# Head and product order of a split-fp32 trunk kernel: meta tokens transposed in one go, a regrouped third weight chunk, another bank for the taps, another table of products

## The chip, the cores and the metric

The kernel runs on one core of a Trainium2 chip. The metric is the device time of one execution in microseconds (us): the median over three timed runs. Lower is better. Where a single execution was profiled, its own time is given beside the span that the profiler saw.

## The reference

One layer of a decoder trunk over 16 learned meta tokens followed by 256 tokens of x, all in fp32, with D = 2048:

```python
h = concatenate([meta, x])                       # 272 x 2048
u = rms_norm(h, g_pre_mix)
z_pool, v, g, gate_a, gate_b = split(u @ w_in)   # 1024, 1024, 1024, 2048, 2048 columns
y_a = causal_multiscale_pool(z_pool, w_grp, scale) @ w_pool_out
c   = causal_depthwise_conv31(v * sigmoid(g), w_dw) + b_dw
y_b = silu(layer_norm(c, ln_g, ln_b)) @ w_conv_out
m = sigmoid(gate_a) * y_a + sigmoid(gate_b) * y_b
h = h + rms_norm(m @ w_o, g_post_mix)
h = h + rms_norm(relu(rms_norm(h, g_pre_mlp) @ w_up)**2 @ w_down, g_post_mlp)
return h[16:]
```

## The kernel before

**How a product is made.** An fp32 product is three matmuls of the type fp32r: the high part of the weights times the high and the low part of the activations, and the low part of the weights times the high part of the activations. The weights come from HBM in blocks of 1 MB (128 x 2048 fp32), issued by SyncE (SP, L733). ScalarE casts a block to its high part (`hi`, L754), VectorE subtracts that from the block (`lo`, L759), and TensorE uses both. `hi` and `lo` have three buffers each, so that a block is cast when the product three places earlier is done on TensorE.

**Which products there are.** After the head come the products of u with the columns of z, v and g ("Z"), the per-group map `grp`, and then a list of words in a table MAIN. A word such as `a13` is a plain product of a block of the stage a (gate_a) with all 256 tokens, 24 matmuls (stages: p pool projection, a and b the gates, c the conv projection, o the output projection). Words such as `a0P5` belong to a set of seven products in the manner of Strassen that stand for eight plain half-products; each is 12 matmuls. Some of the seven need a sum of two weight blocks. The table SUMMED says for which VectorE adds the two loaded blocks (L771); for the others GpSimd (POOL) issues an accumulating DMA from HBM on top of the block that lies in SBUF (L775), called a "bring" here. Other words of MAIN are steps: `fu` makes the token sums of the Strassen sets, `k1` hands two buffers (`raw_k`, in the place of the pooled activations `y`) to the weight loads once the pool projection is done on TensorE, `lnm` and `lnv` are the mean and the variance of the LayerNorm over c, `um8` hands over another buffer (`raw_um`), `OF` prepares the output projection.

**The order of the work.** TensorE takes the products in the order of MAIN. What VectorE, ScalarE, POOL and SP do is put in order ahead of time by a list scheduler (the class Plan) from written costs and due times; every engine then executes its own list in that order. The loads of SP are in the order in which blocks are first used, and a load waits until a buffer is free. VectorE's list mixes splits, sums, gate arithmetic and the 240 instructions of the depthwise conv ("taps", L886, 128x256 each), which must all be done before `lnm`.

**The head.** x comes in four blocks of 512 columns (`load_x`, L407): blocks 0 and 1 are issued by ScalarE's queue, 2 and 3 by SP between the weight chunks. The first two chunks (`raw_103`, `raw_109`) come in four pieces each. TensorE first does 14 dummy transposes (`keep_warm`, L430), one small transpose of g_pre_mix (L401) and 10 more dummies; then `x_tile` (L457) for column tiles k = 0 to 15: two 128x128 transposes of x (L461) and one of 16 meta rows (L462) into one PSUM tile, from which ScalarE (L463) makes the high and VectorE (L464) the low part of 272 columns of u. Between these transposes the loop multiplies the first chunk (`acc_v<-u_um`, L490), three tiles behind. ScalarE and VectorE split chunks 0, 1 and 2 in pieces of 128x256 meanwhile (`pieces_to`, L517), chunk 2 interleaved with chunk 1 in the last half. Four of the squares for the RMS norm (L472) go to odd k from 9 on.

**Rows and taps.** `rows_step` sums the squares over partitions into bank `y0` (L825), VectorE copies them to `rb` (L828); `taps_step` then transposes the rows of parameters into the same bank `y0` (L837) and the taps into `y1` (L841).

## Time and profile before

| | before |
|---|---|
| timed runs | 1197.83, 1196.41, 1196.10 us; median 1196.41 us |
| profiled execution, its own time | 1194.79 us |
| its span in the profile | 1193.0 us |
| mean granted TensorE clock | 0.997 |
| busy time of TensorE matmuls (PE) | 1172.1 us, 6324 instructions |
| busy time of VectorE (DVE) | 1076.1 us |
| busy time of ScalarE (ACT) | 710.4 us |
| busy time of GpSimd (POOL) | 54.6 us |
| DMA | 281.27 MB, 236 GB/s on average |

Busy times are of the whole span. In lists of instructions the first column is the start in us from the span's start, the second the time until the end of the last of the instructions in the row; "x14" at the end is how many instructions the row holds; brackets hold the idle time of the engine ahead of it and what ended it. The head reaches to about 48 us, the products of z, v and g to 161 us, the words of MAIN to 515 us; then come the two MLP products.

### The profile page before, as it was taken

To read this page: it belongs to the slowest core of one execution; us is meant where nothing else is said; L and a number is where in the kernel's file an instruction comes from. 1 tells how busy PE (TensorE), PEld (TensorE's weight loads), DVE (VectorE), ACT (ScalarE), POOL (GpSimd) and SP (SyncE) were. 2 spreads that over 40 slices of the span, in tenths; PEclk is the share of its full clock that TensorE was granted. 3 is DMA by queue.
4 is the path that set the end of the run, shared out by engine and by line. 5 is a ranking of instruction groups with operands and counts; after the bars stand their busy time and mean duration, and the time that the engine had idled before them with its cause. 6 is when DMAs were issued, how large, how long until landed. Compare 5 with 4: busy or idle time off the path is not lost.

```text
span 1193.0 us, 15777 instructions
## 1 busy us (share of the span) xinstructions
PE 1172.1 (98%) x6324; PEld 1013.9 (85%) x6324; DVE 1076.1 (90%) x1160; ACT 710.4 (60%) x718; POOL 54.6 (5%) x55
## 2 busy tenths in 40 slices
PE   9999999899999999999999999999999999999996
PEld 7999998788788878898888888888888888888885
DVE  5799999999988998787989989989999999899856
ACT  6633354565559656557776665666656756656542
POOL 1000000000000000000100000000000000000000
PEclk9999999999999999999999999999999999999998
DMA  9756444889856798549998897997998987979931
GB/s 310 230 177 212 142 141 141 237 258 268 249 187 212 176 388 258 196 128 345 236 342 225 246 317 179 262 309 191 300 276 211 304 239 234 317 181 266 331 140 70
DMA packets 181976, 281.27 MB, mean 236 GB/s; under 512 B 4641, under 2 KB 92129, under 8 KB 180992
## 3 DMA queue, kind: packets, MB, share of 16 engines
q1 hardware_dynamic: 160064, 235.09, 57.7%
q0 software_dynamic: 20688, 43.15, 19.9%
q10 hardware_dynamic: 1152, 2.04, 0.5%
q8 instruction: 49, 0.80, 0.3%
q14 instruction: 23, 0.19, 0.0%
HBM read 276.07 MB, written 4.19 MB: 235 GB/s over the span
## 4 chain that ended last, share of the span: by engine, by line
PE 78%; DVE 9%; DMA 7%; ACT 4%; issue 1%; ACTq 0%; DVEq 0%; SPq 0%
PE bank_u L495 16%; PE acc_up L1850 12%; PE bank_k L1166 11%; PE bank_u L501 8%; PE bank_k L490 7%; PE bank_a L1850 7%; PE bank_b L1850 5%; PE acc_v L490 4%; DVE lo L759 4%; PE acc_v L1166 4%; ACT hi L754 2%; DMA raw_p<-in_w_in_dram 2%; DMA kept<-h 1%; DVE c L886 1%; DVE raw_p L771 1%
## 5 line engine op out<-in xcount | busy, mean ns | idle before, releaser
L495 PE MATMUL bank_u<-m,hi 128*128 128x512 f32 x960 | 329.4, 390 | 0.0
L501 PE MATMUL bank_u<-m,lo 128*128 128x256 f32 x960 | 265.3, 276 | 0.0
L495 PEld LDWEIGHTS bank_u<-m,hi 128*128 128x128 f32 x960 | 180.2, 188 | 37.9
L754 ACT CAST hi<-raw_p 128x2048 fp32r<-128x2048 f32 x66 | 125.9, 1912 | 107.9 <-PE bank_k L1166 28.2
L501 PEld LDWEIGHTS bank_u<-m,lo 128*128 128x128 f32 x960 | 180.2, 188 | 1.6
L1676 DVE TENSOR_TENSOR lo<-raw_m,hi 128x2048 fp32r<-128x2048 f32 x71 | 162.4, 2287 | 15.2 <-ACT hi L1671 14.9
L1671 ACT CAST hi<-raw_m 128x2048 fp32r<-128x2048 f32 x71 | 135.8, 1913 | 52.0 <-PE bank_u L495 18.0
L759 DVE TENSOR_TENSOR lo<-raw_p,hi 128x2048 fp32r<-128x2048 f32 x66 | 150.4, 2287 | 15.6 <-ACT hi L754 15.4
L1850 PE MATMUL acc_up<-hi,forms 128*128 128x512 f32 x440 | 143.1, 390 | 1.0 <-ACT G L1875 1.0
L1671 ACT CAST hi<-raw_h 128x2048 fp32r<-128x2048 f32 x46 | 88.0, 1913 | 51.1 <-PE bank_u L495 32.0
L1676 DVE TENSOR_TENSOR lo<-raw_h,hi 128x2048 fp32r<-128x2048 f32 x46 | 105.2, 2287 | 13.8 <-ACT hi L1671 13.7
L886 DVE SCALAR_TENSOR_TENSOR c<-a,taps,c 128x256 f32<-128x256 f32 x240 | 100.6, 480 | 0.2
L1850 PEld LDWEIGHTS acc_up<-hi,forms 128*128 128x128 f32 x440 | 82.6, 188 | 19.1 <-ACT G L1875 1.4
L490 PE MATMUL bank_k<-u_um,hi 128*128 128x272 f32 x512 | 95.0, 287 | 0.0
L1166 PE MATMUL bank_k<-hi,u_um 128*128 128x512 f32 x272 | 87.2, 391 | 0.7 <-ACT sg L1212 0.7
L1850 PE MATMUL acc_up<-lo,forms 128*128 128x512 f32 x220 | 85.9, 391 | 0.0
L1850 PE MATMUL bank_a<-hi,forms 128*128 128x512 f32 (+1 forms) x256 | 82.0, 383 | 0.0
L490 PEld LDWEIGHTS bank_k<-u_um,hi 128*128 128x128 f32 x512 | 79.9, 188 | 0.0
L490 PE MATMUL bank_k<-u_um,lo 128*128 128x272 f32 x256 | 73.3, 286 | 0.0
L1671 ACT CAST hi<-raw_a 128x2048 fp32r<-128x2048 f32 x23 | 44.0, 1913 | 34.0 <-PE bank_u L495 25.1
L1850 PE MATMUL bank_b<-hi,forms 128*128 128x512 f32 (+1 forms) x200 | 63.4, 381 | 0.0
L1676 DVE TENSOR_TENSOR lo<-raw_a,hi 128x2048 fp32r<-128x2048 f32 x23 | 52.6, 2287 | 11.1 <-ACT hi L1671 11.0
(391 smaller groups left out, 2261.2 us busy)
## 6 DMA issues: line engine op xcount, KB each, us to landing
raw_p<-in_w_in_dram SPq DMA_DIRECT2D x33, 1024.0 KB, 5.2
raw_m<-in_w_up_dram SPq DMA_DIRECT2D x25, 1024.0 KB, 9.7
raw_m<-in_w_down_dram SPq DMA_DIRECT2D x22, 1024.0 KB, 7.9
raw_h<-in_w_down_dram SPq DMA_DIRECT2D x21, 1024.0 KB, 7.7
raw_h<-in_w_up_dram SPq DMA_DIRECT2D x16, 1024.0 KB, 8.6
raw_a<-in_w_down_dram SPq DMA_DIRECT2D x12, 1024.0 KB, 5.7
raw_k<-in_w_in_dram SPq DMA_DIRECT2D x11, 1024.0 KB, 5.8
raw_a<-in_w_up_dram SPq DMA_DIRECT2D x11, 1024.0 KB, 7.1
```

Of the source, the lines that this page charges most:

```text
L490: nc.tensor.matmul(acc, w[:, k[0], cs], act[:, k[1], a, off:], start=first and n == 0, stop=last and n == 2)
L495: nc.tensor.matmul(acc.rearrange("p (a t) -> p a t", a=2)[:, :, ts], hi[:, k[0], cs], act[:, k[1], :, off + ts.start:off + ts.stop], start ...
L501: nc.tensor.matmul(acc[:, :T], lo[:, k[0], cs], act[:, k[1], 0, off:], start=False, stop=stop, skip_group_check=True)
L754: nc.scalar.copy(box["flat"], rooms[q]())
L759: nc.vector.tensor_sub(lo, rooms[q](), f32(box["flat"]))
L771: plan.add("DVE", 2.22, lambda a=at_rooms[0], b=at_rooms[1]: nc.vector.tensor_add(rooms[a](), rooms[a](), rooms[b]()), reads=names, writes ...
L886: nc.vector.scalar_tensor_tensor(C_c()[:, q, :], A_a()[:, q, i:i + T], taps[:, q, i:i + 1], C_c()[:, q, :], op0=ALU.mult, op1=ALU.add)
L1166: nc.tensor.matmul(banks[bank], a_(k, part), box[w_][:, k, :], start=opens and k == 0 and i == 0, stop=ends_ and k == CK - 1 and i == 2, s ...
L1671: nc.scalar.copy(box["flat"], raw_in(room))
L1676: nc.vector.tensor_sub(lo, raw_in(room), f32(box["flat"]))
L1850: nc.tensor.matmul(acc, forms[h][:, f, k, a_, :], box[w_][:, k, cs], start=start and k == 0 and n == 0, stop=stop and k == KH - 1 and n == ...
```

## The change

The change has six parts. Line numbers of the changed kernel stand in the listings of the order below; in the words they are those of the kernel before.

1. The 16 meta transposes leave `x_tile`. A new function `meta_tiles` does all of them at once into one PSUM tile `mt_in`, ahead of the x tiles; VectorE multiplies them with g_pre_mix (128x256), and four casts of ScalarE and four subtractions of VectorE put them into u. The tiles of x are 256 columns wide instead of 272. The dummies behind the transpose of g_pre_mix go from 10 to 4.
2. Chunk 0 comes in five pieces of 1, 1, 2, 2, 2 rows of 128x256. Chunk 2 is loaded right behind x's last block and split in four pieces of 128x512 behind the last x tile (two at k = 13, one at 14, one at 15). The four squares go to k = 5, 7, 9 and 11.
3. The first block of x is issued in two halves, one by ScalarE's queue and one by SP's, ahead of the weight pieces.
4. `taps_step` stands behind the first Z product of g, and both of its transposes go to bank `y1`; the memset of `a` moves to `rows_step`.
5. MAIN has another order of the same products. `lnm` comes 6 units earlier (a unit is 12 matmuls) and `lnv` three words of 4 units behind it, where it was 3 units. The load of h (2 MB, POOL) is a step `h1`.
6. SUMMED is by set: a0P7 and c2P4 are added by VectorE instead of brought, b0P6 is brought instead of added (11 sums and 9 brings, where it was 10 and 10). The token sums of the set c2 have a buffer of their own name and are made at `um8`.

```diff
+DUMMIES = 4
+SQUARES_FROM = 5
 MAIN = (
-    "fu p00 p01 p11 p21 p31 p10 p20 p30 k1 a0P1 a0P5 a12 a13 a0P6 a0P3 a2P1 a0P7 a0P2 a03 a0P4 "
...
+    "p00 p01 fu p11 p10 p20 p30 p21 p31 k1 a0P1 a0P5 a13 a0P6 a12 a0P7 a03 a0P3 a2P1 a0P4 a2P5 "
...
-SUMMED = {"gate0": "56", "gate1": "56", "co": "56", "o": "56", "po": "56"}
+SUMMED = {('gate0', 0): '567', ('gate0', 2): '56', ('gate1', 0): '5', ('co', 2): '564', ('o', 0): '56'}
...
-        pieces = rows if n < FIRST + 1 else 1
+        pieces = rows if n < FIRST else 4 if n == FIRST else 1
...
-        loads = 4 if n < FIRST else 1
+        cuts = ((0, 1, 2, 4, 6, 8), (0, 2, 4, 6, 8))[n] if n < FIRST else (0, rows)
...
-    load_x(nc.scalar, 0)
+    for t, queue in enumerate((nc.scalar, nc.sync)):
+        queue.dma_start(x_in[:, t, :CW], xv[:, t, :CW])
     load_x(nc.scalar, 1)
     for b in range(2, XB):
         open_chunk()
         load_x(nc.sync, b)
+    open_chunk()
...
-    keep_warm(10)
+    keep_warm(DUMMIES)
...
-            nc.tensor.transpose(pt[:, M + t * P:M + (t + 1) * P], x_in[:, t, sl], ident)
-        nc.tensor.transpose(pt[:, 0:M], m_in[:, sl], ident[:M, :M])
+            nc.tensor.transpose(pt[:, t * P:(t + 1) * P], x_in[:, t, sl], ident)
...
+    def meta_tiles():
+        pt = acc_tile("mt_in")[:, :KD * M].rearrange("p (k m) -> p k m", k=KD)
+        for k in range(KD):
+            nc.tensor.transpose(pt[:, k, :], m_in[:, k * P:(k + 1) * P], ident[:M, :M])
+        g0 = cols["g_pre_mix"]
+        mt = tmp.tile([P, KD * M], F32, tag="v", bufs=5, name="mt").rearrange(
+            "p (k m) -> p k m", k=KD)
+        nc.vector.tensor_mul(mt, pt, vecs[:, g0:g0 + KD, None].broadcast_to([P, KD, M]))
+        for ks in (slice(0, K_FIRST), slice(K_FIRST, KD)):
+            for i, (hi, lo) in enumerate(zip(u.meta(ks, 0), u.meta(ks, 1))):
+                src = mt[:, ks.start:ks.stop - 1, :] if i == 0 else mt[:, ks.stop - 1, :]
+                nc.scalar.copy(hi, src)
+                nc.vector.tensor_sub(lo, src, f32(hi))
...
-        pieces_to(k + LEAD + 1 + max(k, 0) * 8 // KD)
+        pieces_to(k + LEAD + 1)
...
-        if k >= HALF[0] and k % 2:
+        if k >= SQUARES_FROM and k % 2 and k < KD - LEAD:
             sq_tile(*squares.pop(0))
+        for _ in range((2, 1, 1)[k - KD + LEAD] if k >= KD - LEAD else 0):
+            opened[FIRST][2].pop(0)()
...
-    steps[3:3] = [("rows",), ("taps",)]
+    steps[3:3] = [("rows",)]
+    steps[1:1] = [("taps",)]
...
-            nc.tensor.transpose(banks["y0"][:, :n_rows], rows[:n_rows, :], ident[:n_rows, :n_rows])
+            nc.tensor.transpose(banks["y1"][:, CW // 2:CW // 2 + n_rows], rows[:n_rows, :],
+                                ident[:n_rows, :n_rows])
```

**TensorE, the start of the program.** Before (`xt` is the PSUM tile of an x tile, `acc_v` the sums of the first chunk):

```order
L430 MATMUL idle<-ident 128x128 x14
L401 MATMUL pv_g_pre_mix<-ident,rows_g_pre_mix 128x16
L430 MATMUL idle<-ident 128x128 x10
L461 MATMUL xt_160<-ident,x_in 128x128 x2
L462 MATMUL xt_160<-ident,m_in 128x16
L461 MATMUL xt_168<-ident,x_in 128x128 x2
L462 MATMUL xt_168<-ident,m_in 128x16
```

and now:

```order
L434 MATMUL idle<-ident 128x128 x14
L403 MATMUL pv_g_pre_mix<-ident,rows_g_pre_mix 128x16
L434 MATMUL idle<-ident 128x128 x4
L482 MATMUL mt_in<-ident,m_in 128x16 x16
L472 MATMUL xt_185<-ident,x_in 128x128 x2
L472 MATMUL xt_192<-ident,x_in 128x128 x2
```

The 16 small transposes stand together behind four dummies, and each x tile is two transposes.

**VectorE, around the first products of the gates.** Before; `lo_2228` belongs to a0P5, `lo_2250` to a12, `lo_2308` to a13, the second sum and `lo_2342` to a0P6, `lo_2326` to a0P3:

```order
L759 TENSOR_TENSOR lo_2228<-raw_p_418,hi_2208 128x2048
L886 SCALAR_TENSOR_TENSOR c<-a,taps,c 128x256 x2
L759 TENSOR_TENSOR lo_2250<-raw_p_417,hi_2244 128x2048
L886 SCALAR_TENSOR_TENSOR c<-a,taps,c 128x256 x14
L759 TENSOR_TENSOR lo_2308<-raw_k_2242,hi_2290 128x2048
L771 TENSOR_TENSOR raw_p_418<-raw_p_418,raw_k_2242 128x2048
L759 TENSOR_TENSOR lo_2326<-raw_k_2242,hi_2310 128x2048
L759 TENSOR_TENSOR lo_2342<-raw_p_418,hi_2328 128x2048
```

and now; `lo_2223` belongs to a0P5, `lo_2245` to a13, the two sums and `lo_2295` and `lo_2314` to a0P6 and a0P7, `lo_2299` to a12:

```order
L793 TENSOR_TENSOR lo_2223<-raw_p_417,hi_2204 128x2048
L923 SCALAR_TENSOR_TENSOR c<-a,taps,c 128x256 x2
L793 TENSOR_TENSOR lo_2245<-raw_p_416,hi_2239 128x2048
L923 SCALAR_TENSOR_TENSOR c<-a,taps,c 128x256 x2
L805 TENSOR_TENSOR raw_p_417<-raw_p_417,raw_k_2237 128x2048
L805 TENSOR_TENSOR raw_p_415<-raw_p_415,raw_k_2237 128x2048
L793 TENSOR_TENSOR lo_2295<-raw_p_417,hi_2279 128x2048
L793 TENSOR_TENSOR lo_2299<-raw_k_2237,hi_2293 128x2048
L793 TENSOR_TENSOR lo_2314<-raw_p_415,hi_2297 128x2048
```

The product that is split from a `raw_k` buffer first was a13, directly from the block; now the first use of `raw_k` is in two sums, for a0P6 and a0P7, and a13 is split from a block that was loaded earlier. POOL's bring for a0P7, which stood ahead of these rows, is gone.

**VectorE, from the mean of the LayerNorm to the sum of its squares.** Before (`v_419` is the mean from bank `y0`, filled at `lnm`; the last `sq` is what `lnv` waits for):

```order
L1009 TENSOR_SCALAR v_419<-bank_y_414 128x256
L1013 TENSOR_TENSOR c<-c,v_419 128x1024 x2
L759 TENSOR_TENSOR lo_3132<-raw_p_418,hi_3101 128x2048
L1020 TENSOR_TENSOR sq<-sq 128x1024
L1024 TENSOR_TENSOR sq<-sq 128x512
L1028 TENSOR_TENSOR sq<-sq 128x256
```

and now:

```order
L1046 TENSOR_SCALAR v_418<-bank_y_413 128x256
L1162 TENSOR_TENSOR ya<-ya,sg_2259 128x512
L1050 TENSOR_TENSOR c<-c,v_418 128x1024
L793 TENSOR_TENSOR lo_3010<-raw_p_417,hi_2991 128x2048
L1050 TENSOR_TENSOR c<-c,v_418 128x1024
L793 TENSOR_TENSOR lo_3043<-raw_p_416,hi_3026 128x2048
L1057 TENSOR_TENSOR sq<-sq 128x1024
L1162 TENSOR_TENSOR ya<-ya,sg_2259 128x512
L1061 TENSOR_TENSOR sq<-sq 128x512
L1162 TENSOR_TENSOR ya<-ya,sg_2259 128x512
L1065 TENSOR_TENSOR sq<-sq 128x256
```

Two splits and three gate sums (`ya`) stand in this stretch, where one split stood.

More of the change, by code (lines that the diff above doesn't have):

```diff
@@ L453, in __getitem__, with meta @@
             return room[:, c0:c0 + L][:, cols_]
+        def meta(self, ks, part):
+            room = self.rooms[ks.start >= K_FIRST]
+            n = ks.stop - ks.start
+            whole = room[:, :2 * (n - 1) * PITCH].rearrange("p (k a c) -> p k a c", a=2, c=PITCH)
+            return whole[:, :, part, :M], room[:, (2 * n - 2 + part) * PITCH:][:, :M]
     u = Tokens((K_FIRST, "um", 0), (KD - K_FIRST, "um8", 3 * LINE))
@@ L1065, in ln_var_step @@
                 [f"sa{h}"] + halves_c(h), (f"sa{h}l",))
-        if any(s[0] == "S" and s[1] == "co" for s in steps):
-            plan.take(form_names("fc"), form_names("fu") + names_d)
-            cs = {f"{h + 1}{t + 1}": (lambda h=h, t=t: C_c()[:, t * QW:(t + 1) * QW, half(h)])
-                  for h in range(2) for t in range(2)}
-            make_forms(K0_f, "fc", cs, {b: halves_c(int(b[1]) - 1) for b in cs})
     FORM = {"7": 0, "5": 1, "6": 2, "3": 3}
@@ L1152, in __init__ @@
             self.bank = {}
-            self.parts = 1 + (sources[stage][1] > 2 * CK)
+            self.parts = 1 + (("N", stage, n0 + 1, 2) in products)
+            self.gives = {}
         def product(self, t, n, m_, a_, names, gives, last):
@@ L1204, in give @@
             n = self.n0
+            self.gives[s] = self.gives.get(s, 0) + 1
+            if self.gives[s] < sum(q[:4] == ("S", self.stage, n, s) for q in products):
+                return
             t, j = {"1": (0, 0), "5": (1, 1), "6": (0, 1), "7": (1, 1)}[s]
@@ L1322, in um8_step, with c_step @@
         loads()
+    def c_step():
+        plan.take([f"q1{b}" for b in BLOCKS], [f"mt{i}" for i in range(2 * NT)] + names_c)
     def o_step():
```

124 lines of the change are left out of this document (81 added, 43 removed), and 8 rows, old and new, of the table MAIN.

## The prediction

> **What bounds the kernel now.** I read the page first: busy times, then the waits of the engine that is busiest, then that engine's timeline at each wait, and then the queue that the wait points to.
>
> ```profile
> PE 1172.1 (98%) x6324; PEld 1013.9 (85%) x6324; DVE 1076.1 (90%) x1160; ACT 710.4 (60%) x718; POOL 54.6 (5%) x55
> ```
>
> TensorE (PE) is busy for 98% of the span, so a change that adds no arithmetic can only gain what PE idles, and what PE does that need not be done. The waits of PE (us in total, times, longest) name the idle time:
>
> ```profile
> PE bank_k L1166 <- DVE lo L759: 4.8, 4, 1.6
> ...
> PE acc_v L490 <- DVE y L983: 0.8, 1, 0.8
> PE xt L461 <- DMA x_in<-in_x_dram: 0.8, 2, 0.4
> PE bank_k L1166 <- ACT sg L1212: 0.7, 1, 0.7
> PE bank_y L837 <- DVE rb L828: 0.5, 1, 0.5
> ```
>
> These 7.6 us lie in the part that the change touches. The four waits for `lo`, 4.8 us, are the largest, and each will have to be read by itself. The MLP from 515 us on is the same code.
>
> **The head.** PE's timeline, and the weight load of a meta transpose from the view of the tile `m_in`:
>
> ```profile
> 1.36 3.25 PE L430 MATMUL idle<-ident 128*128 128x128 f32 x14 [1.36 <-POOL ident masks.py:199]
> ...
> 5.23 1.19 PE L430 MATMUL idle<-ident 128*128 128x128 f32 x8
> ...
> 6.83 0.44 PE L461 MATMUL xt<-ident,x_in 128*128 128x128 f32 x2 [0.41 <-DMA x_in<-in_x_dram]
> ...
> 7.36 0.44 PE L461 MATMUL xt<-ident,x_in 128*128 128x128 f32 x2
> ...
> 10.35 0.41 PE L461 MATMUL xt<-ident,x_in 128*128 128x128 f32 x2 [0.40 <-DMA x_in<-in_x_dram]
> ...
> 12.04 0.23 PE L462 MATMUL xt<-ident,m_in 16*128 16x16 f32 x1
> 12.20 0.52 PE L490 MATMUL acc_v<-u_um,hi 128*128 128x272 f32 x2
> ```
> ```profile
> L462 PEld LDWEIGHTS xt<-ident,m_in x16: 133/134/134, 7.2 to 25.4; 16*128 16x128 f32 x16
> ```
> ```profile
> 7.99 0.50 DVE L464 SCALAR_TENSOR_TENSOR u_um<-xt,vecs,u_um 128x272 fp32r<-128x272 f32 x1 [2.95 <-ACT u_um L463]
> ```
>
> A meta transpose takes 0.16 us of PE (12.04 to 12.20). Twelve stand in the loop behind the first four tiles, where PE has no other wait: 12 x 0.16 = 1.9 us go. The 16 at once cost between 16 x 0.134 = 2.1 us (weight load alone) and 16 x 0.16 = 2.6 us; six dummies fewer pay for about 0.9, so the first x tile starts at some 7.9 instead of 6.83, and x, which came at 6.8, is no longer waited for. Whether its first block by two queues comes sooner is then covered; if that cover went, at most the 0.41 us of this wait would be at stake. Four tiles without meta take 4 x (0.53 - 0.16) = 1.5 us. Beside them stand VectorE's multiplication and four casts and subtractions of at most 0.5 us each (row 7.99 is the nearest, larger form) ahead of the first u; ScalarE and VectorE overlap, so 1.5 to 2.5 us from 7.9, and u of tile 0 is whole at about 10.1 instead of 8.5. The first group of products is late by as much, but before, PE then stood still until 10.35 for x's second block. I put the fifth x tile at 10.9, 0.5 us later. Net **-1.4 us** (bounds -2.2, if the chain hides, to +0.5, if it takes 2.5 us). Chunk 2's four larger pieces come behind the last x tile, three products of a tile ahead of their use, and stand behind nothing on ScalarE and VectorE but the last tile's own parts. The other five edits of the loop (pieces, squares, cuts) move work of engines that do not set PE's pace there, and I cost them at nothing; without that cover each would cost its own time once.
>
> **The taps' bank** removes the wait of L837 for `rb`: the bank is no longer shared, and what is late next is nothing, since the next split was done. **-0.5 us**. In front of `grp` two taps fewer stand before the last `lo` and `y`, by the order; at 0.40 us a tap (row 216.29 below, 14 in 5.64) that is up to 0.8; I take half: **-0.4 us**.
>
> **The first gate products.** PE, SP, POOL, ScalarE, VectorE there:
>
> ```profile
> 218.08 0.50 PE L1166 MATMUL bank_k<-hi,u_um 128*128 128x512 f32 x1 [0.68 <-ACT sg L1212]
> ...
> 223.66 0.39 PE L1166 MATMUL bank_k<-hi,u_um 128*128 128x512 f32 x1
> 225.54 0.50 PE L1166 MATMUL bank_k<-lo,u_um 128*128 128x512 f32 x1 [1.49 <-DVE lo L759]
> ...
> 232.15 0.50 PE L1166 MATMUL bank_k<-lo,forms_k 128*128 128x512 f32 x1 [0.87 <-DVE lo L759]
> ```
> ```profile
> 212.00 1.70 SPq L733 DMA_DIRECT2D raw_k<-in_w_in_dram  x2
> ```
> ```profile
> 209.41 1.37 POOL L775 DMA_DIRECT2D raw_p<-in_w_in_dram  x1 [169.55 <-DVE c L886]
> ```
> ```profile
> 221.25 1.91 ACT L754 CAST hi<-raw_k 128x2048 fp32r<-128x2048 f32 x1 [3.22 <-DMA raw_k<-in_w_in_dram]
> ```
> ```profile
> 216.29 5.64 DVE L886 SCALAR_TENSOR_TENSOR c<-a,taps,c 128x256 f32<-128x256 f32 x14
> 223.20 2.29 DVE L759 TENSOR_TENSOR lo<-raw_k,hi 128x2048 fp32r<-128x2048 f32 x1 [1.27 <-ACT hi L754]
> 225.40 2.28 DVE L771 TENSOR_TENSOR raw_p<-raw_p,raw_k 128x2048 f32<-128x2048 f32 x1
> ```
>
> The wait of 1.49 us is named after VectorE, but ScalarE's row shows the cause: the block `raw_k`, issued at 212.0, as soon as PE was done with the pool projection, was cast from 221.25 on, 9.2 us later. Since 209.41 a bring was on the same DMA engines. Two issue groups show what a load and a bring take, the first where two loads were on the way together with no bring beside them:
>
> ```profile
> raw_p<-in_w_conv_out_dram SPq DMA_DIRECT2D x1, 1024.0 KB, 5.8
> ```
> ```profile
> raw_p<-in_w_in_dram POOLq DMA_DIRECT2D x1, 1024.0 KB, 9.9
> ```
>
> The change takes this bring away, so I put the landing at 212.0 + 5.8 = 217.8 (bounds: 217.0 and, as before, 220.9). But the first user is now a0P6, which needs more than a split: two sums and a `lo`, 2.28 + 2.28 + 2.29 less 0.1 of overlap each, 6.6 us; the cast of ScalarE lies beside the second sum. Behind these wait the `lo` of a12 and a0P7 on VectorE; both have a product of PE as cover. With 0.2 us of start a0P6's `lo` is done at 224.6. PE has done a13, as long as a12 was, at 223.66 and wants `lo` one matmul later, 223.9: a wait of 0.7 in place of 1.49 + 0.87 = 2.36. The 0.68 us for bank `sg` stay, since a13 follows a0P5 in the same bank. **-1.5 us**, with bounds -2.4 (landing at 217.0) and +1.5 (landing at 220.9, the wait then 3.9).
>
> **Two later waits.** At 304 and 425 us:
>
> ```profile
> 304.04 0.50 PE L1166 MATMUL bank_k<-lo,u_um 128*128 128x512 f32 x1 [0.88 <-DVE lo L759]
> ```
> ```profile
> 425.68 0.50 PE L1166 MATMUL bank_k<-lo,m 128*128 128x512 f32 x1 [1.57 <-DVE lo L759]
> ```
> ```profile
> 410.28 1.28 POOL L775 DMA_DIRECT2D raw_p<-in_w_conv_out_dram  x1 [21.96 <-DVE lo L759]
> ```
> ```profile
> 421.39 1.91 ACT L754 CAST hi<-raw_um 128x2048 fp32r<-128x2048 f32 x1 [1.18 <-DMA raw_um<-in_w_o_dram]
> ```
>
> At 425 it is the same picture: c2P4's bring was on its way from 410.28, and the cast of `raw_um` waited for its load. This bring goes too (an addition of 2.28 us on VectorE takes its place, off PE's path), and h's 2 MB come between; **-1.2 us** of 1.57. At 304 two taps of 0.40 fewer stand ahead of the `lo`: **-0.45** of 0.88. Both bounds are 0 and the whole wait.
>
> **What the new order adds.** From the mean to the squares VectorE did:
>
> ```profile
> 348.12 0.42 DVE L1009 TENSOR_SCALAR v<-bank_y 128x256 f32<-128x256 f32 x1 [1.59 <-PE bank_y L1005]
> 348.58 2.36 DVE L1013 TENSOR_TENSOR c<-c,v 128x1024 f32<-128x1024 f32 x2
> 350.85 2.28 DVE L759 TENSOR_TENSOR lo<-raw_p,hi 128x2048 fp32r<-128x2048 f32 x1
> 353.06 1.22 DVE L1020 TENSOR_TENSOR sq<-sq 128x1024 f32<-128x1024 f32 x1
> 354.31 0.69 DVE L1024 TENSOR_TENSOR sq<-sq 128x512 f32<-128x512 f32 x1
> 355.04 0.42 DVE L1028 TENSOR_TENSOR sq<-sq 128x256 f32<-128x256 f32 x1
> ```
>
> Now the list there is 0.42 + 2.36 + 2 x 2.28 + 1.22 + 0.69 + 0.42 and three gate sums of the 128x512 form (0.69): 11.7 us. PE comes to `lnv` four units of 12 matmuls after `lnm`, a unit (218.08 to 223.66 is two) 2.75 us, so after 11. **+0.6 us** (0 to +2, if the second cast waits for a bank). Loads whose buffer comes free only some 8 us ahead of use (b12, b13) would be 1 to 2 us late beside a bring; I find one by the order only at their edges: **+0.3** (0 to +1.5).
>
> Sum: -1.4 - 0.5 - 0.4 - 1.5 - 1.2 - 0.45 + 0.6 + 0.3 = -4.5 us. The profiled execution took 1194.79, so 1190.3; the median of the timed runs lies 1.6 above it, so **1191.9 us**. About 0.2% (2.4 us) is what a measurement of this kernel tells from no change. With all waits gone and nothing added the sum is -8.1; the case's own range is 1189.5 to 1193.8.
>
> **The rivals.** *The load was slow for another reason than the bring.* Then a0P6 waits 3.9 us (+1.5 for -1.5) and the wait at 425 stays: -4.5 + 3.0 + 1.2 = -0.3, 1196.1. For it: `raw_k` is two loads at once. Against it: the pair without a bring, 5.8 us. 11%.
>
> *VectorE falls behind, and `lnv` waits.* All taps must be done 6 units, 16 us, sooner. VectorE's busy time in four stretches' rows:
>
> ```profile
> 224.00:304.00 80.00, 76.80 (x337) 62.91 (x336) 78.39 (x76) 49.65 (x36) 5.12 (x4) 1.00 0.86 255
> 304.00:352.00 48.00, 47.96 (x211) 39.71 (x212) 45.09 (x50) 25.02 (x17) 1.28 (x1) 1.00 0.68 219
> 352.00:424.00 72.00, 72.00 (x326) 59.50 (x325) 63.96 (x55) 53.17 (x60) 2.82 (x3) 1.00 0.69 209
> ```
>
> By the order's counts at the trace's durations VectorE, never waiting, ends the squares about 5.8 us before PE comes to `lnv` (9.2 before). It idled 2% of 224 to 304, 6% of 304 to 352 and 11% of 352 to 424. Of the 162 us from `grp` to `lnv`, 2% cost nothing, 6% (9.7 us) would make PE wait 4 us, 11% (18 us) 12 us: 1195.9 and 1204. Slower than before from 10.3 us idle on. For it: the two sums wait for `raw_k` with only two taps ahead, where 14 stood. Against it: before, half of its idle time came after the taps ran out. 19%, of it 14% slower by over 0.2%.
>
> *The change does not do what it says*: each later `lo` takes over the wait, since VectorE has no time to spare, and only the head and the bank remain, -1.9: 1194.5. 11%.
>
> *PE's clock.* The 14 dummies took 3.25 us, 0.23 each, the eight from 5.23 on 1.19, 0.15 each. If PE stayed at the slow pace through the short meta transposes, as long as it did before (1.36 to some 5.4, 4 us at about half pace), 2 us would be lost: 1193.9. 6%.
>
> [...]
>
> **Numbers.** Forecast 53%, rivals 11, 19, 11 and 6%. Faster by over 0.2%: 53 + 3 + 5 = 61%; slower: 14%; the rest, 25%, within. The range that leaves out 2 in 10 goes from 1188.5 (near -8.1) to 1199.0 (part of the VectorE case).
>
> **What would show it.** PE: L837's wait gone; no wait for `xt`; the first matmul of the second Z product 1.4 us earlier; `raw_k` landed by 218 and one wait under 1 us at a0P6; no wait over 0.5 us at the output projection's first blocks; at `lnv` a wait under 1 us. A wait of 3 us or more at a0P6 or `lnv`, or a first Z product not earlier than before, would make the prediction wrong.

## The result, and the profile after

| | before | after |
|---|---|---|
| timed, median | 1196.47 us (20 runs, 1194.91 to 1201.02) | 1195.78 us (20 runs, 1192.83 to 1198.71) |
| ratio to before, 95% interval | 1 | 0.9989 (0.9979 to 0.9998) |
| profiled execution, own time; span | 1194.79; 1193.0 us | 1195.48; 1193.4 us |
| first matmul of the second Z product | 28.61 us | 25.54 us |
| first product of MAIN | 168.26 us | 164.14 us |
| squares of `lnv` on PE | 356.12 us | 339.44 us |
| end of MAIN (first transpose of h) | 513.50 us | 513.82 us |
| MAIN, from first product to end | 345.24 us | 349.68 us |

By the ratio the kernel became faster by 1.3 us (0.2 to 2.5), which is within 0.2% of no change; 4.5 us were forecast. The median lies in the stated range of 1188.5 to 1199.0, but above the forecast's own case (1189.5 to 1193.8). The table's lower half tells where it went: the head and the products of z, v and g end 4.1 us earlier, and MAIN, which does the same products, takes 4.4 us longer. The MLP behind it differs by some tenths. These are the rows that bound MAIN in the timelines of TensorE, before and after:

```profile
168.26 0.40 PE L1166 MATMUL bank_k<-hi,y 128*128 128x512 f32 x1
...
513.50 0.27 PE L1453 MATMUL ht<-ident,h 128*128 128x128 f32 x1
```
```profile
164.14 0.40 PE L1199 MATMUL bank_k<-hi,y 128*128 128x512 f32 x1
...
513.82 0.38 PE L1524 MATMUL ht<-ident,h 128*128 128x128 f32 x2
```

The busy times of the page after say nothing of this; PE is at 98% in both kernels:

```profile
PE 1171.5 (98%) x6318; PEld 1012.9 (85%) x6318; DVE 1079.1 (90%) x1162; ACT 711.5 (60%) x718; POOL 53.3 (4%) x54
```

The waits of PE after (us in total, times, longest):

```profile
PE bank_k L1199 <- DVE lo L793: 1.7, 2, 1.0
PE bank_k L1199 <- DVE m L1312: 1.5, 1, 1.5
...
PE bank_k L1199 <- DVE sg L1244: 1.1, 2, 0.8
PE acc_v L515 <- ACT hi L338: 0.9, 1, 0.9
PE bank_y L1072 <- DVE sq L1065: 0.9, 1, 0.9
...
PE bank_y L1303 <- DVE sg L1171: 0.7, 1, 0.7
...
PE bank_y L1303 <- DVE m L1312: 0.5, 1, 0.5
```

The four waits for `lo`, 4.8 us, shrank to two of 1.7; the waits for `rb` and for x are gone. In their place stand waits for `m`, `sg` and `sq` (`sg` is a gate's value and sum, `m` the split activations of the output projection, `sq` the squares of the LayerNorm): other tasks of VectorE, at other places. PE's timeline gives the places:

```profile
219.83 0.50 PE L1199 MATMUL bank_k<-lo,forms_u 128*128 128x512 f32 x1
...
265.64 0.50 PE L1199 MATMUL bank_k<-lo,u_um 128*128 128x512 f32 x1 [1.00 <-DVE lo L793]
...
275.22 0.50 PE L1199 MATMUL bank_k<-hi,u_um 128*128 128x512 f32 x1 [0.80 <-DVE sg L1244]
...
339.44 0.48 PE L1072 MATMUL bank_y<-sq,ones 128*128 128x256 f32 x1 [0.88 <-DVE sq L1065]
...
434.88 0.33 PE L1303 MATMUL bank_y<-ident,sg 128*128 128x128 f32 x1 [0.68 <-DVE sg L1171]
...
452.81 0.50 PE L1199 MATMUL bank_k<-hi,m 128*128 128x512 f32 x1 [1.47 <-DVE m L1312]
```

The row at 219.83 has no bracket: a0P6, which was put at 0.7 us of wait, does not wait for a time that the view would show. With three smaller ones that are left out here (0.30 at 233.79, 0.69 at 392.78, 0.55 at 436.09) the new brackets sum to 6.4 us. By the spacing of all matmuls of MAIN, summed over what it has beyond the median of their form, PE lost 7.6 us before and 12.0 after; the difference is the whole 4.4. The known waits went (1.49, 0.87, 0.88 and 1.57, 4.8 us by their brackets), so about 9 us of new loss came (4.8 and 4.4); the new brackets hold 6.4 of it.

Now the start of the program after, PE's timeline; the row `x16` holds the meta transposes:

```profile
5.79 1.29 PE L482 MATMUL mt_in<-ident,m_in 16*128 16x16 f32 x16
7.01 1.09 PE L472 MATMUL xt<-ident,x_in 128*128 128x128 f32 x8
8.98 0.62 PE L515 MATMUL acc_v<-u_um,hi 128*128 128x272 f32 x2 [0.88 <-ACT hi L338]
...
10.62 0.63 PE L472 MATMUL xt<-ident,x_in 128*128 128x128 f32 x2
...
12.40 0.63 PE L472 MATMUL xt<-ident,x_in 128*128 128x128 f32 x2
...
13.65 0.38 PE L472 MATMUL xt<-ident,x_in 128*128 128x128 f32 x2
```

The 16 transposes take 1.2 us together (5.79 to 7.01). A step of the loop, from one x tile to the next, lasts 1.78 us at first (10.62 to 12.40) and then 1.25 (12.40 to 13.65). The stretches of the same execution show why; behind the busy times stands the granted clock:

```profile
5.00:9.00 4.00, 3.12 (x29) 2.53 (x28) 1.42 (x7) 1.42 (x7) 0.00 (x0) 1.00 1.02 343
9.00:13.00 4.00, 4.00 (x17) 3.82 (x18) 3.49 (x10) 2.71 (x8) 0.00 (x0) 0.57 1.08 336
13.00:17.00 4.00, 4.00 (x35) 4.00 (x34) 2.93 (x8) 3.31 (x9) 0.00 (x0) 1.00 1.08 361
```

From 9 to 13 us the clock is 0.57 and PE does 17 matmuls, in the next 4 us 35. Ahead of it lies the wait of 0.88 for the first high part of the weights (`hi`), which ScalarE casts right behind the first u. The loss that the rival on PE's clock (6%) put a price on came in this run, but not in its way: PE had left the slow pace by the x tiles (the row at 7.01, eight transposes in 1.09 us) and fell back to it behind the wait.

### The profile page after: what moved, and what is told of

It reads as the page before. It is cut to its first block, busy times and chain, and to the rows that moved or that the text cites. A ratio compares the mean times of both kernels' runs of the same rounds, so it can differ in the third digit from the quotient of the medians.

```text
span 1193.4 us, 15768 instructions
## 1 busy us (share of the span) xinstructions
PE 1171.5 (98%) x6318; PEld 1012.9 (85%) x6318; DVE 1079.1 (90%) x1162; ACT 711.5 (60%) x718; POOL 53.3 (4%) x54
## 3 DMA queue, kind: packets, MB, share of 16 engines
q10 hardware_dynamic: 1024, 1.78, 0.4%
## 4 chain that ended last, share of the span: by engine, by line
PE 76%; DVE 14%; DMA 4%; issue 3%; ACT 2%; DVEq 0%; POOL 0%; ACTq 0%; POOLq 0%
PE bank_u L520 18%; PE acc_up L1921 13%; PE bank_u L526 9%; PE bank_a L1921 7%; PE bank_k L1199 7%; DVE lo L793 6%; PE bank_k L515 6%; PE bank_b L1921 5%; DMA raw_p<-in_w_in_dram 3%; PE acc_v L515 3%; DVE c L923 3%; PE acc_v L1199 3%; PE acc_up L520 1%; ACT hi L788 1%; DVE raw_p L805 1%
## 5 line engine op out<-in xcount | busy, mean ns | idle before, releaser
L788 ACT CAST hi<-raw_p 128x2048 fp32r<-128x2048 f32 x70 | 134.1, 1915 | 114.5 <-PE bank_k L1199 34.3
L793 DVE TENSOR_TENSOR lo<-raw_p,hi 128x2048 fp32r<-128x2048 f32 x70 | 160.0, 2290 | 16.9 <-ACT hi L788 16.7
```

Source lines behind the costliest of these rows:

```text
L788: nc.scalar.copy(box["flat"], rooms[q]())
L793: nc.vector.tensor_sub(lo, rooms[q](), f32(box["flat"]))
```

## The experiments

Two theories stood at the start. The first: head and table are separate; the head gains more than forecast, and the table makes new waits of its own. The rival: the head's gain is given back in MAIN whatever the table does, since VectorE and the loads set MAIN's end. Times below are medians, with their ratio to before and its 95% interval; before was timed anew beside each group of runs, so differences between groups are taken from the ratios. MAIN is read from one profiled execution of each kernel. The changed kernel without and with eight more dummies, which have the same MAIN, took 349.68 and 348.29 us for it, so a difference of MAIN under some 1.5 us says little by itself. "The dummies" are eight more transposes ahead of the first product.

### The head alone, the table alone

The new head with the old table (MAIN and SUMMED of before; `h1` behind `OF`, where it was inside):

```diff
 MAIN = (
-    "p00 p01 fu p11 p10 p20 p30 p21 p31 k1 a0P1 a0P5 a13 a0P6 a12 a0P7 a03 a0P3 a2P1 a0P4 a2P5 "
...
+    "fu p00 p01 p11 p21 p31 p10 p20 p30 k1 a0P1 a0P5 a12 a13 a0P6 a0P3 a2P1 a0P7 a0P2 a03 a0P4 "
...
+    "c2P3 T11 T10 c2P2 c2P7 T01 o21 c2P4 T20 T31 o20 T21 T30 OF h1 o22 o0P1 o0P5 o23 o13 o0P6 o0P3 "
...
-SUMMED = {('gate0', 0): '567', ('gate0', 2): '56', ('gate1', 0): '5', ('co', 2): '564', ('o', 0): '56'}
+SUMMED = {}
```

> The changed head and taps step with the product table and SUMMED of before. Theory A (the head gains, the new table gives it back): TensorE reaches the first MAIN product near 164.1 us as in the change (168.3 before), the waits in MAIN are those of before (0.7, 1.5, 0.9, 0.9, 1.6 us), and the execution is some 4 us shorter than before, about 0.9966 of it. Theory B (TensorE runs into VectorE, which has no time to spare, whatever the table): the waits in MAIN grow by 3 us or more over those of before, and the time stays within 1 us of before.

Measured: 1194.3 us, 0.9984 (0.9975 to 0.9993). The second Z product starts at 26.37, MAIN at 164.99 us, and MAIN takes 348.34. This fits neither theory: the time is 1.9 us shorter by the ratio, and MAIN is 3.1 us longer than before.

The old head with the new table:

```diff
-    keep_warm(DUMMIES)
+    keep_warm(10)
...
-            nc.tensor.transpose(pt[:, t * P:(t + 1) * P], x_in[:, t, sl], ident)
+            nc.tensor.transpose(pt[:, M + t * P:M + (t + 1) * P], x_in[:, t, sl], ident)
+        nc.tensor.transpose(pt[:, 0:M], m_in[:, sl], ident[:M, :M])
...
```

> The new product table and SUMMED with the head and taps step of before. Theory A: the waits at a0P5 to a0P6, at 304 and at 425 us go (about 5.5 us), the new waits of the change (9 to 10 us between 230 and 455 us) stand at the same products, and the execution is 3 to 4.5 us longer than before, about 1.003 of it. Theory B: the new waits are smaller here, since TensorE comes 4 us later to each product while VectorE's work is the same; the time is within 1 us of before.

Measured: 1197.57 us, 1.0012 (1.0003 to 1.0021). MAIN starts at 168.15, as before, and takes 347.63 us. So the table with its smaller edits costs 1.4 us by the ratio, and the head gains, though in the head-only run PE was at half pace from the program's start to about 14 us (its eight x transposes took 1.97 us, where the change's took 1.09; 18 matmuls from 9 to 13 us). MAIN is 2.0 us shorter here than in the whole change: behind the earlier head the waits for VectorE are longer (`lo` at 265.64 1.00 us against 0.29 here, `sq` at `lnv` 0.88 against 0.48, `lo` at 392.78 0.69 against 0.21), the sign of the second theory. The next question is whether a few dummies ahead of the first product keep the pace.

### Dummies in front of the first u

The changed kernel, with eight dummies behind the first x tiles:

```diff
+        if k == 0:
+            keep_warm(8)
```

> The change, with 8 dummy transposes of 128x128 ahead of the first product of the head, where TensorE waited 0.88 us. If the half pace of TensorE from 9 to 12.6 us (granted clock 0.85 to 0.89 in those stretches) comes from too little work of TensorE in the 3 us ahead of it (16 short transposes and the wait), it is gone: clock 1.00 in every stretch, and the second Z product starts about 1.3 us earlier, near 24.2. [...]

Measured: 1193.97 us, 0.9975 (0.9965 to 0.9985); the second Z product starts at 24.39, and MAIN takes 348.29. And the same with the old table:

```diff
+        if k == 0:
+            keep_warm(8)
...
-SUMMED = {('gate0', 0): '567', ('gate0', 2): '56', ('gate1', 0): '5', ('co', 2): '564', ('o', 0): '56'}
+SUMMED = {}
```

> The changed head with the 8 dummies, with the product table and SUMMED of before. Theory A with the clock's explanation: 4 + 1.3 = 5.3 us shorter than before, about 0.9956. Theory B: within 1 us of before.

Measured: 1191.51 us, 0.9963 (0.995 to 0.9977); second Z product at 23.53, 5.1 us ahead of before, and MAIN 348.11. PE's timeline of this run, where the eight dummies stand in the place of the wait:

```profile
6.54 1.09 PE L472 MATMUL xt<-ident,x_in 128*128 128x128 f32 x8
7.47 1.04 PE L434 MATMUL idle<-ident 128*128 128x128 f32 x8
...
9.67 0.38 PE L472 MATMUL xt<-ident,x_in 128*128 128x128 f32 x2
9.81 0.49 PE L515 MATMUL acc_v<-u_um,hi 128*128 128x272 f32 x2
...
10.64 0.38 PE L472 MATMUL xt<-ident,x_in 128*128 128x128 f32 x2
```
```profile
9.00:13.00 4.00, 4.00 (x33) 3.93 (x33) 3.63 (x11) 3.44 (x11) 0.00 (x0) 1.00 1.07 335
```

At full pace a step of the loop is 0.97 us (9.67 to 10.64). Of the nine kernels profiled with the dummies, six reach the second Z product by 24.6 us; the three with the bring, with the later steps and with h last (below) take until 25.4 to 26.8. But what parts the six from the three lies ahead of the dummies: in the six the eight x transposes before them take 1.09 us, as in the first row above, and in the three 1.97, as in the head-only run. With h last:

```profile
7.61 1.97 PE L472 MATMUL xt<-ident,x_in 128*128 128x128 f32 x8
```

So no profile shows that the dummies bring PE to full pace sooner. What the profiles show is that PE, once at full pace, fell back at the first products in none of the six (in the run above 33 matmuls stand from 9 to 13 us, at clock 1.00), and that it did in the change without dummies (17, at 0.57). With the dummies the times are 1.7 (new table) and 2.5 us (old table) shorter by the ratios; how much of that is the kept pace, and how much how often a run starts at full pace, is open.

### The gate's bring given back

a0P7 is again brought by POOL, everything else as with the dummies:

```diff
-SUMMED = {('gate0', 0): '567', ('gate0', 2): '56', ('gate1', 0): '5', ('co', 2): '564', ('o', 0): '56'}
+SUMMED = {('gate0', 0): '56', ('gate0', 2): '56', ('gate1', 0): '5', ('co', 2): '564', ('o', 0): '56'}
```

> The change with the 8 dummies, and with a0P7 brought by POOL again (SUMMED of that set '56'). If the bring is what slowed the two raw_k loads, the first of them takes 8.5 us or more again (5.2 in the change), and a0P6 waits 2.5 to 4 us for its lo where it waited 0.2; the time is 2 to 3.5 us longer than with the dummies alone. If the pair of loads was slow or fast for another reason, the landing stays near 5.2 us and the time within 1 us.

Measured: 1197.32 us, 0.9998 (0.9988 to 1.0009), by the ratios 2.8 us above the same kernel without the edit; MAIN takes 351.87 us, 3.6 more. DMA groups of 206 to 214 us after, and of 203 to 218 us in this run (KB each, median us from issue to landing):

```profile
raw_k<-in_w_in_dram SPq DMA_DIRECT2D x2, 1024.0 KB, 7.1
```
```profile
raw_k<-in_w_in_dram SPq DMA_DIRECT2D x2, 1024.0 KB, 10.0
raw_p<-in_w_in_dram POOLq DMA_DIRECT2D x1, 1024.0 KB, 10.0
```

The pair `raw_k` takes 10.0 beside a bring of 10.0, and 7.1 without it (the median of two is their mean: the first of the pair lands after 8.9 us beside the bring and after 5.2 without, the second, issued right behind, after 11.2 and 9.0). PE pays at a0P6:

```profile
221.00 0.49 PE L1201 MATMUL bank_k<-hi,forms_u 128*128 128x512 f32 x1 [1.44 <-ACT hi L790]
...
223.59 0.80 PE L1201 MATMUL bank_k<-lo,forms_u 128*128 128x512 f32 x1 [2.10 <-DVE lo L795]
```
```profile
218.00:224.00 6.00, 2.46 (x9) 1.54 (x9) 6.00 (x9) 4.95 (x3) 0.16 (x1) 0.84 0.55 201
224.00:228.00 4.00, 4.00 (x10) 3.06 (x10) 4.00 (x3) 0.55 (x1) 1.13 (x1) 0.50 0.54 72
```

Two waits, 3.5 us, and behind them 4 us at clock 0.50, in which PE does 10 matmuls (17 in the next 4 us, at 0.89). The bring is the cause of the gate waits, and these two cost more than themselves.

### What makes the new waits in MAIN

First VectorE's load: with the dummies, every third tap on 16 of its 256 columns only.

```diff
+                    e = i + (16 if i % 3 == 0 else T)
...
-                        C_c()[:, q, :], A_a()[:, q, i:i + T], taps[:, q, i:i + 1], C_c()[:, q, :],
+                        C_c()[:, q, :e - i], A_a()[:, q, i:e], taps[:, q, i:i + 1],
```

> The change with the 8 dummies, and with every third tap of the depthwise conv cut to its first 16 of 256 columns (that part of the convolution is left out): 80 of 240 instructions become about 0.2 us shorter, some 16 us of VectorE's time, in unchanged order. If VectorE's time makes the waits between 230 and 340 us (bank and lo waits of 0.46, 0.53, 1.10 us and 1.05 us at lnv in the run with the dummies), those up to 290 us go and the time falls by 2 us or more against that run. If they come from where an instruction stands in VectorE's list or from the DMA, they stay, and the time falls by less than 1 us. The waits at 431, 433 and 448 us, behind the last tap, should stay under both.

Measured: 1191.72 us, 0.9955 (0.9938 to 0.9972). By the ratios that is 2.4 us less than with the dummies alone, as the first case has it, but MAIN takes 347.34 us, only 0.95 less (348.29). Of the 2.4 us between the two spans 1.2 stand in the MLP, whose code is the same and whose length lies between 679.1 and 680.9 us in the profiles. In MAIN the waits at 232.84 (for a bank's `sg`) and 263.64 (for `lo`) are gone and the one at `lnv` falls from 1.05 to 0.30 by the spacing, but the next wait for a bank's `sg`, 0.94 with the dummies alone, grew:

```profile
PE bank_k L1202 <- DVE sg L1247: 2.0, 1, 2.0
```

Everything from 389 us on is as it was. In MAIN, VectorE's time explains about 1 of the 9 us.

Then, with the dummies, steps of the table were moved: `lnv` a word later, the steps of the gates' token sums for the output projection (T) and `OF` among other products.

```diff
-    "b0P7 lnv b03 b12 b0P2 b13 b0P4 b0P3 k0r b30 b31 b02 um8 c01 c2P1 c2P5 c00 c2P6 c2P3 c2P7 "
-    "c2P2 c2P4 T00 T01 c10 CD T31 T30 o0P1 c11 T20 o23 T11 T10 o20 o21 T21 OF o22 o0P5 o0P6 o0P3 "
+    "b0P7 b03 lnv b12 b0P2 b13 b0P4 b0P3 k0r b30 b31 b02 um8 c01 c2P1 c2P5 c00 c2P6 c2P3 c2P7 "
+    "c2P2 c2P4 T00 T01 c10 CD T31 T30 o0P1 c11 T20 o23 T21 o20 T11 T10 o22 OF o21 o0P5 o0P6 o0P3 "
```

> The change with the 8 dummies, lnv one plain product later (behind b03), and the transposes T21 ahead of o20, T11 and T10 between o20 and o22, OF ahead of o21. If the waits at lnv (1.05 us) and at the transposes and the first product behind them (0.84, 0.71, 1.66 us) are chains of VectorE and ScalarE that are longer than the products put between, they shrink to under 1 us in all, and the time is 3 us shorter than with the dummies alone, near 1191. If VectorE is late as a whole, the waits reappear at the next users and the gain is under 1 us.

Measured: 1195.85 us, 0.9994 (0.9982 to 1.0006), by the ratios 2.3 us longer than with the dummies alone, where 3 shorter were hoped for. The wait at `lnv` is gone, but in the profiled execution a wait of 3.8 us at 400.8 came, of a kind that no other profile has:

```profile
PE acc_v L1201 <- ACT mts L1250: 3.8, 1, 3.8
```

The planner writes new lists for all engines when words change places, so this run does not tell what the moved steps cost. Nor is its profile typical: that execution took 1199.61 us, 3.8 above the median, and 8 of the 12 took under 1196.1.

The sums without the new order: old table, new head and dummies, and a0P7 and c2P4 added by VectorE.

```diff
-SUMMED = {}
+SUMMED = {('gate0', 0): '567', ('co', 2): '564'}
```

> The changed head with the 8 dummies and the product table of before, with the one difference that a0P7 and c2P4 are summed on VectorE instead of brought. If the two brings alone made the waits at a13 and a0P6 (1.62 and 1.03 us in the run without this edit) and at o21 (2.10 us and the stretch at half pace behind it), these go, and the time is 3 to 5 us shorter than that run, near 1188; the new order of products is then not needed for it. If two more sums of 2.3 us on VectorE cost as much as they save, the waits move to the next lo and the time stays within 1 us.

Measured: 1200.64 us, 1.0032 (1.0019 to 1.0044); MAIN takes 357.00 us.

```profile
PE bank_y L1074 <- DVE sq L1067: 3.1, 1, 3.1
PE bank_k L1201 <- DVE lo L795: 2.7, 3, 1.4
```

Here waits for VectorE stand all along MAIN; `lnv` alone waits 3.1. The additions cost 8.9 us of MAIN in the old order (357.00 against 348.11). Some 5 us of the 357.00 go with the clock, which is 0.96 from 350 to 430 us and 0.98 from 430 to 520 (0.04 x 80 + 0.02 x 90). In the new order, where b0P6 is brought, the same two additions stand in a MAIN of 348.29: it is the new order that makes them affordable.

Next h. In the changed kernel its 2 MB are issued at 407.58 (before: 423.74), among the first loads of w_o. With the dummies, its DMA is made to wait until a later part of m is there:

```diff
-        plan.add("POOL", 6.0, lambda: nc.gpsimd.dma_start(K0_h1(), xv), writes=("h1",))
+        plan.add("POOL", 6.0, lambda: nc.gpsimd.dma_start(K0_h1(), xv),
+                 reads=("m21",), writes=("h1",))
```

> The change with the 8 dummies, and with h's 2 MB load issued only when T21's tokens are split (near 446 us, it was near 407). If h's load slows the loads of the output projection beside it (12 us each in the change), the late split behind them is what holds VectorE's gate sums and so the transposes T11 and T10: these loads then take 5 to 8 us, the two waits (0.84 and 0.71 us over the pace) go, and the time is 1 to 1.5 us shorter. If the gate sums are late for another reason, the loads get faster and the waits stay. The wait near 450 us (1.66 us) should stay in both: there a weight sum stands ahead of the split of m in VectorE's list.

Measured: 1190.55 us, 0.9949 (0.9936 to 0.9962), by the ratios 3.1 us below the run with the dummies alone, where 1 to 1.5 were expected. DMA groups of 403 to 414 us, after and in this run:

```profile
h<-in_x_dram POOLq DMA_DIRECT2D x1, 2048.0 KB, 12.5
...
raw_um<-in_w_o_dram SPq DMA_DIRECT2D x1, 1024.0 KB, 12.2
```
```profile
raw_um<-in_w_o_dram SPq DMA_DIRECT2D x1, 1024.0 KB, 5.3
```

A load of w_o beside h takes 12.2 us, without it 5.3. MAIN falls from 348.29 to 345.36 us. The waits for `sg` and `m` from 430 to 453 are gone; the one for `m` at about 450 was expected to stay, and why it went is not settled, because the edit also changed the written order. ScalarE shows it, in the run with the dummies alone and in this one:

```profile
425.84 0.59 ACT L1250 COPY og<-bank_k 128x512 f32<-128x512 f32 x1 [4.75 <-PE bank_k L1201]
426.32 1.91 ACT L790 CAST hi<-raw_um 128x2048 fp32r<-128x2048 f32 x1
```
```profile
419.99 1.92 ACT L790 CAST hi<-raw_um 128x2048 fp32r<-128x2048 f32 x1 [0.78 <-ACT m L1313]
421.80 0.58 ACT L1250 COPY og<-bank_k 128x512 f32<-128x512 f32 x1
```

The cast of `raw_um` now stands ahead of the copy `og`, which waits for PE, and no longer behind it. The 3 us belong to h's place; how much of it is the late load itself and how much the list that the planner then wrote stays open. One new wait of 0.9 us came, at 474.7. A second try puts h behind all of m:

```diff
-                 reads=("m21",), writes=("h1",))
+                 reads=("m21", "gmix"), writes=("h1",))
```

> The run with the 8 dummies and h later, with h's load issued only behind that of g_mix (near 455 to 465 us). With h at 434 us the blocks loaded beside it between 437 and 462 took 13 to 18 us each, and one product near 474 waited 1.03 us for its lo. If h's load is what that wait comes from, it goes and the time is about 1 us shorter again, near 1189.5, 0.994 of before; if the two brings and g_mix make it, the wait stays and the time is that of the run before within 0.5 us.

Measured: 1190.28 us, 0.9954 (0.994 to 0.9969). The wait at 474 is gone, MAIN is 344.88. The medians and the ratios do not tell it from the run before, and its profiled execution was at half pace in the head (eight x transposes in 1.97 us, second Z product at 26.77).

Last, the smaller edits of the change (buffers, steps and written costs that came with the new table, here with the old table and the old head; the new table's own step `k0r`, which hands two more buffers to the weight loads, is not among them and was not run by itself):

```diff
-    keep_warm(DUMMIES)
+    keep_warm(10)
...
-    "p00 p01 fu p11 p10 p20 p30 p21 p31 k1 a0P1 a0P5 a13 a0P6 a12 a0P7 a03 a0P3 a2P1 a0P4 a2P5 "
...
+    "fu p00 p01 p11 p21 p31 p10 p20 p30 k1 a0P1 a0P5 a12 a13 a0P6 a0P3 a2P1 a0P7 a0P2 a03 a0P4 "
...
+    "c2P3 T11 T10 c2P2 c2P7 T01 o21 c2P4 T20 T31 o20 T21 T30 OF h1 o22 o0P1 o0P5 o23 o13 o0P6 o0P3 "
...
-SUMMED = {('gate0', 0): '567', ('gate0', 2): '56', ('gate1', 0): '5', ('co', 2): '564', ('o', 0): '56'}
+SUMMED = {}
```

> The program of the change with the head, the taps step and the product table of before: all that is left are its smaller edits (token sums of c2 at um8, h's load as a step, written costs). From TensorE's first MAIN product to h's first transposes before took 345.2 us; the old table behind the new head took 348.1 to 348.3. If the earlier head makes those 3 us (VectorE cannot follow), the stretch takes 345 to 346 us here and the time is that of before within 1 us. If the smaller edits make them, it takes 348 us and the time is 2 to 3 us longer than before.

Measured: 1198.13 us, 1.0018 (1.0006 to 1.003), and MAIN 347.61 us where before has 345.24. The same waits stand at the same products, but they are longer: 5.6 us for `lo` instead of 4.8, and 0.7 for `hi`, which before did not have. About half of the 2.4 us stands at the output projection's first product, where the waits are 0.74 and 1.82 us instead of 1.57. Against it the kernel of before with the parts 1 to 4 of the change and the dummies, and nothing else:

```diff
+DUMMIES = 4
...
-    keep_warm(10)
+    keep_warm(DUMMIES)
...
+    meta_tiles()
...
+        if k == 0:
+            keep_warm(8)
...
-    steps[3:3] = [("rows",), ("taps",)]
+    steps[3:3] = [("rows",)]
+    steps[1:1] = [("taps",)]
```

> The kernel before with nothing but the changed head, the taps step and the 8 dummies. If the earlier head costs MAIN 3 us, this runs like the run with the dummies and the old table: about 4.4 to 5 us shorter than before, 0.996. If the smaller edits cost them, this is 3 us shorter again, near 0.9935.

Measured: 1189.93 us, 0.9944 (0.9931 to 0.9957). The second Z product starts at 23.82, MAIN at 162.44, and MAIN takes 345.29 us, the length of before to 0.05:

```profile
162.44 0.40 PE L1198 MATMUL bank_k<-hi,y 128*128 128x512 f32 x1
...
507.73 0.38 PE L1485 MATMUL ht<-ident,h 128*128 128x128 f32 x2
```

In the kernel of before an earlier head costs MAIN nothing, and the theory that MAIN gives it back whatever the table falls. With the new table it gives back a part: MAIN takes 347.63 us at the old head, 349.68 at the new one and 348.29 there with the dummies. Beside the run with the same head and dummies, the old table and the smaller edits (348.11) these edits cost 2.8 us, of which 1.7 are a stretch of 4 us at clock 0.58 behind the output projection's waits; at the old head, without such a stretch, 2.4. Which of them does it was not told apart. And the new order itself, with the sums and with h in its new place, neither gains nor loses: at the old head MAIN takes 347.63 us with it and 347.61 without.

Three versions beat both kernels by about the same, and their intervals overlap: before with the new head (0.9944), the changed kernel with h later (0.9949) and with h last (0.9954).

## Why the prediction was right and wrong, step by step

**The head**: forecast -1.4, measured -3.1 in the profiled run, and -5.1 where PE kept its pace. The mechanism was right, the term was mis-sized: a meta transpose inside the loop was put at 0.16 us, the distance to the next matmul, and the fifth x tile at 0.5 us later than before; at full pace it came 0.7 sooner (9.67 against 10.35). Per step of the loop the gain is more. Before, PE's timeline has these x transposes, nine steps apart, with no wait between them:

```profile
13.06 0.38 PE L461 MATMUL xt<-ident,x_in 128*128 128x128 f32 x2
25.06 0.38 PE L461 MATMUL xt<-ident,x_in 128*128 128x128 f32 x2
```

That is 1.33 us a step; at full pace it is now 0.97. So a meta transpose between large ones cost 0.36 us, not 0.16, and twelve cost 4.4 us, not 1.9: the distance behind it does not hold what it does to the pair of x transposes ahead, which went from 0.31 us to 0.14 (9.67 to 9.81 above). Sixteen in a row took 1.2 us, 0.075 each, below the bound of 2.1 that was worked out from weight loads of 0.134: in the row the loads still take 0.138 in the median (0.135 at the least), but start 0.06 apart, one beside the other. Against this stood the clock: the change comes 1.2 us later to the second Z product than the same kernel with dummies, and 2.0 later than the best run with this head.

**The clock rival**: worked out as 2 us, and a loss of that size came. As it was put, PE would stay at the slow pace through the short meta transposes. The head-only run did so, from the start to about 14 us; the change left the slow pace before its x tiles and fell back from 9.5 to 12.9 us, at clock 0.50. The prediction's own times (first x tile at 7.9, u whole at 10.1) hold a wait of PE ahead of the first product; what it did not price is the clock behind this wait. The full pace also did not come at the same time in every run: with the same head and the same dummies, six profiles did the eight x transposes in 1.09 us and three in 1.97. What sets the time was not shown.

**The taps' bank and `grp`**: the wait for `rb` (0.5) is gone and the wait ahead of `grp` fell from 0.8 to 0.4, as forecast. With the head that makes the 4.1 us at the start of MAIN.

**The gates**: forecast -1.5 (its own terms, 0.7 in place of 2.36, make -1.7), measured -2.4. The load came at 213.05, 5.2 us after its issue (forecast 5.8), and a0P6's `lo` was in time. The bring given back shows that the bring was the cause, so the rival of another reason (11%) falls. **The waits at 304 and 425** are gone whole, 2.4 us where 1.65 was forecast. These three steps were right in sign and place, and too small in size.

**"What the new order adds"** failed. It was put at +0.9 (`lnv` 0.6, loads 0.3) and measured at about +9. `lnv` was nearly right, 0.9 by the bracket. The rest was looked for in loads at their edges and in `lo` alone. But an engine that does the same tasks in another order is late in other tasks: the banks' sums, the gate values, the splits of m. And one transfer had been seen and passed over: "h's 2 MB come between" stood in the step on the wait at 425, without a price. It cost about 3 us with the list that came with it. The smaller edits were not looked at as a step at all. They cost 2.4 us at the old head, but with the old table, and mostly at products where the change has no wait; that they are in its 9 us is not shown. By single runs, h's place accounts for 3 us and VectorE's time (most of the wait at `lnv` among it) for 1. Some 5 us of the 9 stay unexplained, and with them the wait for a bank at 275, which grew to 2.0 when VectorE had less to do. The sum also took the head's gain to pass through MAIN whole; with the new table 0.7 to 2.0 us of it came back as longer waits for VectorE.

**The rival that VectorE falls behind and `lnv` waits** (19%) came only as its mild form: `lnv` waits 0.9, and shortening every third tap (18 us of VectorE's busy time) gains 1 us in MAIN. **That the change does not do what it says** (11%, the waits only change place) is, for MAIN, what happened: 4.8 us went and 9 came. Its price of 1194.5 is within 1.3 us of the median, though by luck: the head gained more and MAIN lost more than in its sum.

## What to carry to other kernels

Where a planner writes the lists of several engines, forecast a new order by the total of idle time it moves, not by the waits it removes: removed waits can be read from the trace, the new ones stand at tasks that did not wait before, and small edits beside the order have a price of their own (2.4 us here with the old table). A transfer that changes its place deserves a row of its own: put its size beside the loads issued in the 12 us around it. And before a change is judged as one, run its parts: here the head on the kernel of before, with eight dummies, is worth 6.7 us by its ratio, and all of it together 1.3, or 3.0 with the dummies.

## What the runs showed of the hardware

**A stall of PE can be followed by half clock**, also in the middle of the kernel. In the run with the new head, the dummies and the old table, two waits (0.57 and 1.83 us) from 417 to 421.5 left PE busy for 2.1 of 4.5 us, and the next row is at 0.58:

```profile
417.00:421.50 4.50, 2.10 (x11) 1.33 (x10) 4.42 (x5) 4.50 (x3) 0.73 (x1) 1.00 1.07 397
421.50:425.50 4.00, 4.00 (x12) 3.09 (x11) 4.00 (x5) 1.73 (x3) 0.00 (x0) 0.58 1.01 417
```

12 matmuls stand in those 4 us, and 21 in the 4.5 behind, at 1.00. So this pair of waits costs some 1.7 us more than its brackets. A pair as long need not: with the smaller edits at the old head, 0.74 and 1.82 us at the same product are followed by 19 matmuls at clock 1.00:

```profile
428.60:432.60 4.00, 4.00 (x19) 3.33 (x18) 4.00 (x5) 2.42 (x3) 0.00 (x0) 1.00 1.02 420
```

Nor did single waits of 1.00 and 1.47 us (265.64 and 452.81 after; 18 matmuls at clock 1.00 in the 4 us from 266 and from 453), of 1.99 (shorter taps; clock 1.00 from 250 to 350) and of 2.20 (the sums in the old order, at 213.67; clock 1.00 from 162 to 250) bring half clock. Behind waits of 3.1 us (the sums in the old order), 3.8 (the later steps) and 3.5 (the bring given back, a pair) the clock fell each time: it is 0.96 from 350 to 430 us in the first two, and 0.50 from 224 to 228 in the third. What tells the pair that was followed by half clock from the one that was not is not shown by these runs. The stretch in the head of the change (0.57 from 9 to 13 us) follows a wait of 0.88 us only, ahead of which PE did the short meta transposes and eight of x.

**The clock column does not show the half pace at the program's start.** In the head-only run it reads 1.00 from 9 to 13 us with 18 matmuls, and in the run of the same head with dummies 1.00 with 33; the count of matmuls tells them apart, the clock does not. The head-only run:

```profile
9.00:13.00 4.00, 4.00 (x18) 3.56 (x16) 3.81 (x13) 3.30 (x10) 0.00 (x0) 1.00 1.06 325
```

**A small transpose between large ones was dear here**: 0.36 us for one of 16 rows in a step with a pair of 128x128, 0.075 when 16 stood in a row.
